# Down projection by Strassen's seven products, with gate and up taken in pairs of column blocks

## The chip, the cores and the metric

The kernel runs on one core of a Trainium2 chip. A core has TensorE (PE in the profile), which multiplies 128x128 stationary by 128x512 moving operands into PSUM; VectorE (DVE), ScalarE (ACT) and GpSimd (POOL) for everything elementwise; and SyncE (SP), whose queue issues all the DMAs of this kernel. The metric is the device time of one execution in microseconds; a time given for a kernel is the median of its runs.

## What is computed

A decoder block over 1024 tokens of 1024 channels, in float32: a gated mixer of pooling and sparse attention, a cross-attention over 256 memory tokens, and a SwiGLU feed-forward layer with 2816 inner columns. The change touches the last alone:

```python
def _swiglu(h, w_gate_up, w_down):
    g, u = jnp.split(h @ w_gate_up, 2, axis=-1)
    return (jax.nn.silu(g) * u) @ w_down
# in reference():
h = _rmsnorm(x, norm_ffn_pre)
x = x + _rmsnorm(_swiglu(h, w_gate_up, w_down), norm_ffn_post)
```

`w_gate_up` is 1024 x 5632 and `w_down` is 2816 x 1024.

## The kernel before

**Numbers in two parts.** TensorE is fed with operands split into a rounded high part and the rest (`split`, line 369: ScalarE copies to the rounded type, VectorE subtracts). A product is three matmuls: high x high, high x low, low x high. So every operand costs one pass on ScalarE and one on VectorE before PE can use it.

**The order of the work.** No instruction is issued where it is written. `Recorder` collects all operations with their dependences; `schedule` then runs a list scheduler with a cost table and writes out one fixed order for each engine's queue. In its table a 128x512 matmul costs 227 ns, a VectorE operation 130 ns and 1.06 ns for each element of a row, and a DMA ends 1300 ns, its bytes at 360 GB/s and another 1300 ns after its issue. At every step it takes the operation that can start first, and among equals the one recorded first. Buffers are rings named by tag: `b` (42 slots of 4 KB a partition, for nearly everything), `ld` (4, raw loads), `wraw` (3, raw weights), `whi`/`wlo` (2 each), `ps1` (4 PSUM banks) and `ps2` (2 pairs of banks). An operation that needs a slot of `b` may be placed at most `AHEAD` = 700 records (`SHORT` = 200 where set) ahead of the oldest one not yet placed, and a ring keeps room for tiles that were recorded earlier (`KEEP`).

**Gate and up** (`gate_up`, line 1195) go over 22 blocks `f` of 128 columns, each by Strassen's seven products in Winograd's form over halves of rows (gate, up), channels and tokens. h3, the normed input, is held for the whole stage as seven operands in both parts, 28 slots of `b`. A block is 7 products of 12 matmuls on three banks `A`, `B`, `C`; `B` and `C` are read by VectorE between two products that accumulate onto the same bank (`u2`, `u3`, `c22`), then `c21 = silu(gate) * up` of the first 512 tokens and `c12` of the last 512 are stored to DRAM in `aTd`. The weight operands of block `f + 1` are made while block `f` runs (`get`, `gu_units`: two loads into `wraw`, four sums, four splits, five slots of `b` and two more for the sums). For the first four blocks they are made far earlier, kept in DRAM (`unitd`, `store`, `fetch`), and the products that use A11 and A12 are done ahead (`gu_first`).

**Down** (line 1239 on) goes over pieces of 2, 4, 4, 4, 4 and 4 of the 22 blocks. In each, both parts of the piece's `w_down` rows (128x1024) and activations (`at`, from `aTd`) stay in slots; for each of 8 token tiles `b` and 2 column halves `n`, PE runs 3 matmuls for each block of the piece into one bank, and VectorE adds the 128x1024 result onto `acc[b]`. In the last piece each half is added, multiplied by the gain `g6`, squared and summed on ScalarE (`jf`), scaled by the root on GpSimd (`mef`, `rf`), added to the residual (`x2r`) and stored.

Of the kernel before, what the change touches and what calls it, by code (L numbers as in the profile page):

```python
# [340 lines left out]
def hybrid_block_kernel(ctx: ExitStack, tc: tile.TileContext, x, mem, norm_mix_pre, norm_mix_post,  # L341
# [544 lines left out]
    def store(f):  # L886

        for j, t in enumerate(gu_units(f)):
            v = f32(t) if len(t.shape) == 3 else f32(t).rearrange("p a c m -> p (a c) m")
            nc.sync.dma_start(unitd[f, j], v)  # L890

    def fetch(f, part):

        ts = []
        nc.ahead = nc.SHORT
        for j in (range(2), range(2, 7))[part]:
            if part == 0:
                t = nc.tile(sb, [P, KC, P], F32R, name=f"uw{f}{j}", tag=("whi", "wlo")[j], bufs=2)
                v = f32(t)
            else:  # L900
                t = slot([P, 2, 4, P], F32R, f"uw{f}{j}")
                v = f32(t).rearrange("p a c m -> p (a c) m")
            nc.sync.dma_start(v, unitd[f, j])
# [164 lines left out]
    for b in range(NB):  # L1068
        mg = nc.tile(sb, [P, KC, P], F32, name=f"mg{b}", tag="ld", bufs=LD)
        nc.sync.dma_start(mg, mgd[:, :, b * P:(b + 1) * P].rearrange("k d t -> d k t"))  # L1070
        mgh, mgl = slot([P, KC, P], F32R, f"mgh{b}"), slot([P, KC, P], F32R, f"mgl{b}")
        split(mgh, mgl, mg, scale=0.5)
        o = bank2([P, 2, 512], f"y{b}")
        tok_gemm(o, lambda c: (mgh[:, c], mgl[:, c]), wo, KC)
        nxt = close(o, x, x1d, b, g2, g3, h2T, "a")
        if pend:
            pend()
        pend = nxt
        if b % 2:
            store(b // 2)  # L1080
    pend()


    aTd = nc.tile(dr, [NF, P, 2, 512], F32, name="aTd", tag="aTd", dram=True)
# [100 lines left out]
    def gu_first(f, W):  # L1185

        A = bank([P, 512], f"ga{f}")
        m = slot([P, 2, 512], F32, f"gm{f}")
        prod(A, W["A11"], "B11", True)
        nc.scalar.activation(m[:, 0], A, AF.Copy)  # L1190
        prod(A, W["A12"], "B21", False)
        nc.scalar.activation(m[:, 1], A, AF.Silu)
        return m[:, 0], m[:, 1]

    def gate_up(f, W, head=None):
        A, B, C = (bank([P, 512], f"g{x}{f}") if head is None or x != "a" else None for x in "abc")
        (m1, u2), (u3, c22), (c12, c21) = ([t[:, j] for j in range(2)] for t in [
            nc.tile(sb, [P, 2, 512], F32, name=f"g{x}{f}", tag="ld", bufs=LD) for x in "muv"])
# [24 lines left out]

    def get(f):
        if f < FIRST:
            return sums(*fetch(f, 1))
        ts = gu_units(f)
        return dict(**own(*ts[:2]), **sums(*ts[2:]))

    head = {f: gu_first(f, own(*fetch(f, 0))) for f in range(FIRST)}  # L1230
    nxt = get(0)
    for f in range(NF):
        cur, nxt = nxt, get(f + 1) if f + 1 < NF else None
        gate_up(f, cur, head.get(f))


    g6 = gain(norm_ffn_post, "g6")
    acc = [None] * NB
    pieces = [range(0, 2)] + [range(f, f + 4) for f in range(2, NF, 4)]
    for fs in pieces:  # L1240
        f0 = fs[0]
        aT, wd = {}, {}
        for f in fs:
            wd[f] = wsplit(wload(w_down[f * P:(f + 1) * P, :], f"wd{f}"), f"wd{f}", keep=True)
            at = nc.tile(sb, [P, 2, 512], F32, name=f"at{f}", tag="ld", bufs=LD)
            nc.sync.dma_start(at, aTd[f])
            nc.ahead = nc.SHORT
            aT[f] = slot([P, 2, 512], F32R, f"aTh{f}"), slot([P, 2, 512], F32R, f"aTl{f}")
            split(*aT[f], at)
            nc.ahead = nc.AHEAD  # L1250
        last = fs[-1] == NF - 1
        for b in range(NB):
            h, t = divmod(b, 4)
            qs = slice(t * P, (t + 1) * P)
            if last:
                o = [bank([P, 512], f"dn{f0}{b}{n}") for n in range(2)]
            else:
                o2 = bank2([P, 2, 512], f"dn{f0}{b}")
                o = [o2[:, n] for n in range(2)]
            for n in range(2):  # L1260
                ns = slice(n * 512, (n + 1) * 512)
                for f in fs:
                    mm3(o[n], aT[f][0][:, h, qs], aT[f][1][:, h, qs], wd[f][0][:, ns], wd[f][1][:, ns],
                        f == fs[0], f == fs[-1])
            if f0 == 0:
                acc[b] = slot([P, D], F32, f"acc{b}")
                nc.vector.tensor_copy(acc[b], o2.rearrange("p n f -> p (n f)"))
            elif not last:
                nc.vector.tensor_tensor(acc[b], o2.rearrange("p n f -> p (n f)"), acc[b], op=OP.add)
            else:  # L1270
                xb = load(x2d[b * P:(b + 1) * P, :], f"x2r{b}")
                ms, z = [], slot([P, D], F32, f"zf{b}")
                for n in range(2):
                    ns = slice(n * 512, (n + 1) * 512)
                    nc.vector.tensor_tensor(acc[b][:, ns], o[n], acc[b][:, ns], op=OP.add)
                    nc.vector.tensor_tensor(z[:, ns], acc[b][:, ns], g6[:, ns], op=OP.mult)
                    m_ = small([P, 1], F32, f"ms{b}{n}")
                    junk = nc.tile(sb, [P, 512], BF, name=f"jf{b}{n}", tag="bf", bufs=2)
                    nc.scalar.activation(junk, acc[b][:, ns], AF.Square, scale=1.0 / 32.0, accum_out=m_)
                    ms.append(m_)  # L1280
                me = small([P, 1], F32, f"mef{b}")
                nc.gpsimd.tensor_scalar(me, ms[0], ms[1], EPS, op0=OP.add, op1=OP.add)
                r = small([P, 1], F32, f"rf{b}")
                nc.gpsimd.tensor_tensor(r, me, mhalf, op=OP.pow)
                for n in range(2):
                    ns = slice(n * 512, (n + 1) * 512)
                    nc.vector.scalar_tensor_tensor(z[:, ns], z[:, ns], r, xb[:, ns], op0=OP.mult, op1=OP.add)
                    nc.sync.dma_start(out[b * P:(b + 1) * P, ns], z[:, ns])

    with tc.manual_schedule():  # L1290
        nc.emit()
# [29 lines left out]
```

## Time and profile before

| | before |
|---|---|
| median of 3 runs | 1612.32 us (1612.13 to 1615.33) |
| the profiled execution, its own time | 1611.7 us |
| its span, first to last instruction | 1609.9 us |
| PE busy, share of the span | 97% |
| DVE busy | 66% |
| ACT busy | 34% |
| DMA moved | 213.16 MB, mean 132 GB/s |

The span is what the trace shows; the rest of the profiled execution's time lies around it. A busy share says how long an engine had an instruction in work. On PE matmuls overlap, so that the listed duration of one is longer than the distance to the next. The granted clock of PE is shown in parts of its full 2.4 GHz. A line number doesn't tell operations apart here, since all are issued through one helper (L139); they are told apart by the names of their tiles.

### The profile page before, as it was taken

The numbers are of one execution on the slowest core, as the hardware profiler recorded it, in microseconds if no ns is written. First come the engines' busy times: TensorE is split into PE (matmuls) and PEld (weight loads), VectorE is DVE, ScalarE is ACT, GpSimd is POOL, SyncE is SP. The second block draws the span as 40 slices with busy tenths as digits, with TensorE's granted clock in tenths as the row PEclk, the third lists the DMA queues.
The fourth block names the chain that finished last, engine by engine and source line by source line (L and its number), as shares of the span: only waits on it lengthen the run. The fifth ranks groups of instructions, "written<-read, shape, count | busy, mean of one in ns | idle before, by whom it ended". The sixth has DMA issues, their size and how long they took to land.

```text
span 1609.9 us, 20252 instructions
## 1 busy us (share of the span) xinstructions
PE 1569.6 (97%) x7590; PEld 1315.9 (82%) x7590; DVE 1054.8 (66%) x1769; ACT 554.4 (34%) x950; POOL 210.1 (13%) x311
## 2 busy tenths in 40 slices
PE   5999999998999999999999999999999999999998
PEld 5877888887888887778899878888888888888886
DVE  6699888989633776468755785755566654644436
ACT  6532111122533655235436661322232222211102
POOL 6055000001232342001103220000000000000001
PEclk9999999999999999999999999999999999999999
DMA  7222412453743232389953356322222225533104
GB/s 224 65 66 68 123 53 66 147 185 116 233 124 92 65 113 79 128 299 370 377 205 106 105 190 216 105 79 80 91 79 83 95 79 162 198 105 105 53 15 157
DMA packets 183683, 213.16 MB, mean 132 GB/s; under 512 B 8600, under 2 KB 141472, under 8 KB 183584
## 3 DMA queue, kind: packets, MB, share of 16 engines
q1 hardware_dynamic: 183584, 211.85, 40.5%
q8 instruction: 60, 0.98, 0.3%
q14 instruction: 39, 0.32, 0.1%
HBM read 148.63 MB, written 63.45 MB: 132 GB/s over the span
## 4 chain that ended last, share of the span: by engine, by line
PE 84%; DVE 7%; issue 4%; DMA 2%; POOL 1%; ACT 1%; SPq 0%; DVEq 0%; POOLq 0%; ACTq 0%
PE dn L139 14%; PE gb L139 11%; PE gc L139 7%; PE ga L139 7%; PE o_q L139 5%; PE o_ga L139 5%; PE o_gp L139 5%; PE o_pa L139 4%; PE y L139 4%; PE po L139 3%; PE lg L139 3%; PE z L139 3%; PE qm L139 3%; PE ap L139 3%; PE pt L139 2%
## 5 line engine op out<-in xcount | busy, mean ns | idle before, releaser
L139 DVE TENSOR_SCALAR_CACHE_REDUCE tja<-score,canda 128x384 bf16<-128x384 f32 (+1 forms) x186 | 165.6, 942 | 0.9
L139 PE MATMUL dn<-h_wd,aTh 128*128 128x512 f32 x352 | 136.8, 389 | 0.0
L139 PE MATMUL dn<-l_wd,aTh 128*128 128x512 f32 x352 | 136.8, 389 | 0.0
L139 PE MATMUL dn<-h_wd,aTl 128*128 128x512 f32 x352 | 136.6, 389 | 0.0
L139 DVE TENSOR_TENSOR acc<-dn,acc 128x1024 f32<-128x1024 f32 (+1 forms) x48 | 50.2, 1047 | 111.6 <-PE dn L139 110.9
L139 POOL TENSOR_SCALAR mef<-ms,ms 128x1 f32<-128x1 f32 x8 | 2.4, 298 | 643.1 <-ACT jf L139 643.1
L139 PEld LDWEIGHTS dn<-h_wd,aTl 128*128 128x128 f32 x352 | 66.1, 188 | 13.8
L139 PEld LDWEIGHTS dn<-l_wd,aTh 128*128 128x128 f32 x352 | 66.1, 188 | 13.8
L139 PEld LDWEIGHTS dn<-h_wd,aTh 128*128 128x128 f32 x352 | 66.1, 188 | 13.5
L139 ACT ACTIVATE h<-s 128x1024 fp32r<-128x1024 f32 x44 | 46.5, 1062 | 82.8 <-DVE s L139 69.1
L139 DVE TENSOR_TENSOR l<-s,h 128x1024 fp32r<-128x1024 f32 x44 | 53.7, 1224 | 31.9 <-PE gc L139 28.1
L139 POOL TENSOR_SCALAR L<-L,ri 128x128 f32<-128x128 f32 (+7 forms) x64 | 48.7, 765 | 175.5 <-DVE ri L139 144.1
L139 PE MATMUL lg<-kTh,qq 128*128 128x512 f32 (+2 forms) x192 | 58.7, 355 | 1.9 <-DVE nn L139 1.3
L139 ACT ACTIVATE aTh<-at 128x1024 fp32r<-128x1024 f32 x22 | 22.8, 1052 | 104.4 <-PE dn L139 94.1
L139 PE MATMUL po<-T,Vh 128*128 128x512 f32 x144 | 55.7, 412 | 2.6 <-DVE T L139 2.5
L139 DVE CUSTOM_DVE_ANT_0 L<-lg,mb 128x256 f32<-128x256 f32 (+1 forms) x64 | 25.5, 402 | 47.8 <-PE lg L139 41.3
L139 DVE TENSOR_TENSOR T<-pt,T 128x512 fp32r<-128x512 f32 x72 | 47.8, 683 | 11.9 <-ACT T L139 11.7
L139 ACT ACTIVATE T<-pt 128x512 fp32r<-128x512 f32 x72 | 40.6, 595 | 34.8 <-PE pt L139 32.4
L139 PE MATMUL y<-h_wo,mgh 128*128 128x512 f32 x128 | 50.4, 394 | 1.4 <-ACT h_wo L139 1.4
L139 ACT ACTIVATE h_wg<-r_wg 128x1024 fp32r<-128x1024 f32 x22 | 23.3, 1061 | 80.2 <-PE ga L139 74.9
L139 PE MATMUL o_ga<-hTh,h_wga 128*128 128x512 f32 x128 | 51.0, 398 | 0.0
L139 POOL TENSOR_TENSOR mb<-Bn,mask 128x1024 f32<-128x1024 f32 (+1 forms) x16 | 34.8, 2174 | 123.8 <-DMA qd<-qh 114.3
(401 smaller groups left out, 4618.1 us busy)
## 6 DMA issues: line engine op xcount, KB each, us to landing
uw<-unitd SPq DMA_DIRECT2D x28, 512.0 KB, 6.0
r_wg<-in_w_gate_up_dram SPq DMA_DIRECT2D x22, 512.0 KB, 4.0
r_wu<-in_w_gate_up_dram SPq DMA_DIRECT2D x22, 512.0 KB, 3.9
aTd<-gv SPq DMA_DIRECT2D x44, 256.0 KB, 2.0
r_wd<-in_w_down_dram SPq DMA_DIRECT2D x22, 512.0 KB, 4.2
at<-aTd SPq DMA_DIRECT2D x22, 512.0 KB, 4.8
qq<-qd SPq DMA_DIRECT2D x32, 256.0 KB, 4.5
r_wpa<-in_w_proj_attn_dram SPq DMA_DIRECT2D x16, 512.0 KB, 4.4
```

The source lines that it names most:

```text
L139: op.emit = lambda: fn(*args, **kw)
```

## The change

Down becomes seven products as well, over halves of the tokens, of DFF (blocks 0 to 10 and 11 to 21) and of the output columns. Each product runs over 11 blocks `k`; for each, it loads one 128x512 block of activations (or of a sum of them) and one of `w_down` (or of a sum of them), splits both at once, and runs 3 matmuls onto each of four banks, one for each tile of 128 tokens. P2 accumulates in the banks of P1 (`A`), P7 and P4 in those of P6 (`B`), and P3 in those of P5 (`C`). P3 runs tile by tile, with all its 11 operands in SBUF, and each tile's closing work stands between.

Gate and up take the blocks in the order 0, 11, 1, 12, and so on. The result tile `c12`, `c21` moves from the `ld` ring to a slot of `b`. After a pair (k, k + 11) four sums of its activations are formed in place on VectorE and stored to DRAM (`act_sums`), next to the blocks that are used as they are; after the first block of a pair four sums of the two `w_down` rows are formed in place and stored (`down_sums`). The diff, cut to its core:

```diff
+    KF = NF // 2
+    ORDER = [k + KF * j for k in range(KF) for j in range(2)]
...
-            nc.tile(sb, [P, 2, 512], F32, name=f"g{x}{f}", tag="ld", bufs=LD) for x in "muv"])
+        (m1, u2), (u3, c22) = ([t[:, j] for j in range(2)] for t in [
+            nc.tile(sb, [P, 2, 512], F32, name=f"g{x}{f}", tag="ld", bufs=LD) for x in "mu"])
+        v = slot([P, 2, 512], F32, f"gv{f}")
+        c12, c21 = v[:, 0], v[:, 1]
...
-        nc.sync.dma_start(aTd[f, :, 0], c21)
+        nc.sync.dma_start(actd["A12" if f >= KF else "A11"][f % KF], c21)
...
-        nc.sync.dma_start(aTd[f, :, 1], c12)
+        if f >= KF:
+            nc.sync.dma_start(actd["A22"][f % KF], c12)
+        return c21, c12
...
+    def act_sums(k, first, second):
+        (A11, A21), (A12, A22) = first, second
+        for n, dst, a, b, op in (("S3", A11, A11, A21, OP.subtract), ("S1", A21, A21, A22, OP.add),
+                                 ("S2", A22, A22, A11, OP.subtract), ("S4", A12, A12, A22, OP.subtract)):
+            nc.vector.tensor_tensor(dst, a, b, op=op)
+            nc.sync.dma_start(actd[n][k], dst)
+
+    def down_sums(k):
+        r = [wload(w_down[f * P:(f + 1) * P, :].rearrange("p (n c) -> p n c", n=2), f"wdr{f}") for f in (k, k + KF)]
+        (B11, B12), (B21, B22) = ([t[:, j] for j in range(2)] for t in r)
+        for n, dst, a, b in (("T1", B11, B12, B11), ("T3", B12, B22, B12), ("T2", B22, B22, B11), ("T4", B21, B21, B22)):
+            nc.vector.tensor_tensor(dst, a, b, op=OP.subtract)
+            nc.sync.dma_start(wdnd[n][k], dst)
...
+    for i, f in enumerate(ORDER):
+        cur, nxt = nxt, get(ORDER[i + 1]) if i + 1 < NF else None
+        got[f] = gate_up(f, cur, head.get(f))
+        if f >= KF:
+            act_sums(f - KF, got.pop(f - KF), got.pop(f))
+        else:
+            down_sums(f)
...
+    SIDE = {"P1": ("A11", "B11"), "P6": ("S2", "T2"), "P2": ("A12", "B21"), "P7": ("S3", "T3"),
+            "P5": ("S1", "T1"), "P4": ("A22", "T4"), "P3": ("S4", "B22")}
+
+    def operands(p, k):
+        a, b = SIDE[p]
+        raw = nc.tile(sb, [P, 2, 512], F32, name=f"dr{p}{k}", tag="ld", bufs=LD)
+        nc.sync.dma_start(raw[:, 0], actd[a][k])
+        if b in wdnd:
+            nc.sync.dma_start(raw[:, 1], wdnd[b][k])
+        else:
+            f, n = k + (KF if b[1] == "2" else 0), int(b[2]) - 1
+            nc.sync.dma_start(raw[:, 1], w_down[f * P:(f + 1) * P, n * 512:(n + 1) * 512])
+        nc.ahead = nc.SHORT
+        hi, lo = slot([P, 2, 512], F32R, f"dh{p}{k}"), slot([P, 2, 512], F32R, f"dl{p}{k}")
+        split(hi, lo, raw)
+        nc.ahead = nc.AHEAD
+        return hi, lo
...
+    def product(p, o, first):
+        for k in range(KF):
+            w = operands(p, k)
+            for t in range(NT):
+                dstep(o[t], w, t, first and k == 0, k == KF - 1)
...
+    A = [bank([P, 512], f"dA{t}") for t in range(NT)]
+    B2 = [bank2([P, 2, 512], f"dB{j}") for j in range(2)]
+    B = [B2[j][:, n] for j in range(2) for n in range(2)]
+    product("P1", A, True)
+    M = [slot([P, 2, 512], F32, f"dm{j}") for j in range(2)]
+    m1 = [M[j][:, n] for j in range(2) for n in range(2)]
+    for t in range(NT):
+        nc.scalar.activation(m1[t], A[t], AF.Copy)
+    product("P6", B, True)
+    for t in range(NT):
+        out_tile(t)
+        nc.vector.tensor_tensor(acc[t][:, half[1]], B[t], m1[t], op=OP.add)
+    product("P2", A, False)
...
+    product("P7", B, False)
...
+    C = [bank([P, 512], f"dC{t}") for t in range(NT)]
+    product("P5", C, True)
...
+    product("P4", B, False)
...
+    ws = [operands("P3", k) for k in range(KF)]
+    for t in range(NT):
+        done(NT + t, 1)
+        done(NT + t, 0)
+        done(t, 0)
+        for k in range(KF):
+            dstep(C[t], ws[k], t, False, k == KF - 1)
+        a = acc[t][:, half[1]]
+        nc.vector.tensor_tensor(a, C[t], a, op=OP.add)
+        done(t, 1)
```

`dstep` is the three matmuls of one token tile; `done(b, n)` is the closing work of one column half of an output tile, with the same operations as before; `out_tile` takes the slot of `acc`.

## Rows read from the trace of the kernel before

**Rows 1.** The page's first part: busy us (share of the span), instructions.
```profile
PE 1569.6 (97%) x7590; PEld 1315.9 (82%) x7590; DVE 1054.8 (66%) x1769; ACT 554.4 (34%) x950; POOL 210.1 (13%) x311
```
**Rows 2.** Windows: stretch, length, busy PE, PEld, DVE, ACT, POOL, clock, DMA share, GB/s.
```profile
600.00:650.00 50.00, 48.96 (x245) 39.93 (x244) 31.76 (x73) 24.15 (x43) 12.16 (x10) 1.00 0.20 66
...
940.00:956.00 16.00, 13.92 (x63) 10.51 (x61) 15.46 (x18) 12.35 (x23) 4.73 (x5) 1.00 0.48 172
...
1030.00:1363.00 333.00, 333.00 (x1471) 275.74 (x1470) 193.53 (x252) 92.77 (x121) 0.00 (x0) 1.00 0.29 92
1363.00:1602.80 239.80, 239.70 (x1058) 198.15 (x1056) 121.15 (x124) 47.34 (x67) 5.99 (x14) 1.00 0.31 107
```
**Rows 3.** The chain that ended last, from 1340 us: start, length, what.
```profile
1360.62 2.72 PE gc L139 x12
1363.34 228.49 PE dn L139 x1008
```
**Rows 4.** Groups of PE: busy us, mean ns; one of down's three alike.
```profile
L139 PE MATMUL dn<-h_wd,aTh 128*128 128x512 f32 x352 | 136.8, 389 | 0.0
```
**Rows 5.** Timeline of PE: start us, length; first and last matmul of down.
```profile
1363.17 0.39 PE L139 MATMUL dn<-h_wd,aTh 128*128 128x512 f32 x1
...
1602.31 0.39 PE L139 MATMUL dn<-h_wd,aTl 128*128 128x512 f32 x1
```
**Rows 6.** Timeline of DVE in one block of gate and up.
```profile
1153.03 0.68 DVE L139 TENSOR_TENSOR s<-r_wg,s 128x512 f32<-128x512 f32 x1
...
1161.87 1.22 DVE L139 TENSOR_TENSOR l<-s,h 128x1024 fp32r<-128x1024 f32 x1 [1.75 <-PE gc L139]
...
1164.82 0.69 DVE L139 TENSOR_TENSOR gu<-gb,gm 128x512 f32<-128x512 f32 x1 [1.12 <-PE gb L139]
```
**Rows 7.** DMA from 1030 to 1363 us; an issue's row ends with us to landing.
```profile
DMA packets 36803, 30.65 MB, mean 92 GB/s; under 512 B 1200, under 2 KB 30896, under 8 KB 36786
...
aTd<-gv SPq DMA_DIRECT2D x35, 256.0 KB, 2.0
```
**Rows 8.** DMA from 684 to 805 us, the most crowded stretch.
```profile
DMA packets 30817, 42.17 MB, mean 349 GB/s; under 512 B 1396, under 2 KB 22270, under 8 KB 30809
...
mg<-mgd SPq DMA_DIRECT2D x8, 512.0 KB, 8.4
...
unitd<-l_wg SPq DMA_DIRECT2D x4, 512.0 KB, 9.3
```
**Rows 9.** Groups of DVE, then of ACT, from 1363 us to the end.
```profile
L139 DVE TENSOR_TENSOR aTl<-at,aTh 128x1024 fp32r<-128x1024 f32 x21 | 25.5, 1218 | 0.0
...
L139 DVE SCALAR_TENSOR_TENSOR zf<-zf,rf,x2r 128x512 f32<-128x512 f32 x16 | 11.3, 745 | 1.2 <-POOL rf L139 1.2
L139 DVE TENSOR_TENSOR acc<-dn,acc 128x512 f32<-128x512 f32 x16 | 11.1, 692 | 12.6 <-PE dn L139 11.9
...
L139 ACT ACTIVATE aTh<-at 128x1024 fp32r<-128x1024 f32 x20 | 20.7, 1051 | 100.9 <-PE dn L139 94.1 <-DMA at<-aTd 6.8
```
**Rows 10.** Timeline of SP's queue, two loads of down's second piece.
```profile
1387.52 0.33 SPq L139 DMA_DIRECT2D r_wd<-in_w_down_dram  x1
1388.65 0.32 SPq L139 DMA_DIRECT2D at<-aTd  x1
```
**Rows 11.** DMA issues from 1363 us to the end.
```profile
at<-aTd SPq DMA_DIRECT2D x20, 512.0 KB, 4.9
...
aTd<-gv SPq DMA_DIRECT2D x1, 256.0 KB, 5.5
```
**Rows 12.** DMA from 1387 to 1400 us, those loads and six more.
```profile
DMA packets 1030, 3.78 MB, mean 291 GB/s; under 512 B 111, under 2 KB 111, under 8 KB 1029
```
**Rows 13.** Timeline of PE where matmuls of two banks alternate.
```profile
645.01 0.40 PE L139 MATMUL o_pa<-atl,h_wpa 128*128 128x512 f32 x1
645.25 0.39 PE L139 MATMUL po<-T,Vh 128*128 128x512 f32 x1
```

More of the change, by code (lines that the diff above doesn't have):

```diff
@@ L902, in fetch @@
                 v = f32(t).rearrange("p a c m -> p (a c) m")
-            nc.sync.dma_start(v, unitd[f, j])
+            nc.sync.dma_start(v, unitd[ORDER.index(f), j])
             ts.append(t)
@@ L1079, in hybrid_block_kernel @@
         if b % 2:
-            store(b // 2)
+            store(ORDER[b // 2])
     pend()
-    aTd = nc.tile(dr, [NF, P, 2, 512], F32, name="aTd", tag="aTd", dram=True)
     KVm = [slot([P, D], F32R, f"{n}n{w}_") for n in "KV" for w in "hl"]
@@ L1221, in gate_up @@
         nc.vector.tensor_tensor(c12, c12, c22, op=OP.mult)
-        nc.sync.dma_start(aTd[f, :, 1], c12)
+        if f >= KF:
+            nc.sync.dma_start(actd["A22"][f % KF], c12)
+        return c21, c12
+    actd = {n: nc.tile(dr, [KF, P, 512], F32, name=f"act{n}", tag=f"act{n}", dram=True)
+            for n in ("A11", "A12", "A22", "S1", "S2", "S3", "S4")}
+    wdnd = {n: nc.tile(dr, [KF, P, 512], F32, name=f"wdn{n}", tag=f"wdn{n}", dram=True)
+            for n in ("T1", "T2", "T3", "T4")}
+    def act_sums(k, first, second):
[10 more added lines that the diff above has]
+            nc.sync.dma_start(wdnd[n][k], dst)
     def get(f):
-        if f < FIRST:
+        if f in ORDER[:FIRST]:
             return sums(*fetch(f, 1))
@@ L1228, in get @@
         return dict(**own(*ts[:2]), **sums(*ts[2:]))
[L1230 to L1234, printed above, removed]
-    g6 = gain(norm_ffn_post, "g6")
[L1238 to L1288, printed above, removed]
@@ new lines, in hybrid_block_kernel @@
+    head = {f: gu_first(f, own(*fetch(f, 0))) for f in ORDER[:FIRST]}
+    nxt = get(ORDER[0])
+    got = {}
+    for i, f in enumerate(ORDER):
[5 more added lines that the diff above has]
+            down_sums(f)
+    g6 = gain(norm_ffn_post, "g6")
+    NT = 4
+    acc = {}
+    SIDE = {"P1": ("A11", "B11"), "P6": ("S2", "T2"), "P2": ("A12", "B21"), "P7": ("S3", "T3"),
+            "P5": ("S1", "T1"), "P4": ("A22", "T4"), "P3": ("S4", "B22")}
@@ new lines, in dstep @@
+    def dstep(o, w, t, first, last):
+        hi, lo = w
+        q = slice(t * P, (t + 1) * P)
+        nc.tensor.matmul(o, hi[:, 0, q], hi[:, 1], start=first, stop=False, skip_group_check=True)
+        nc.tensor.matmul(o, hi[:, 0, q], lo[:, 1], start=False, stop=False, skip_group_check=True)
+        nc.tensor.matmul(o, lo[:, 0, q], hi[:, 1], start=False, stop=last, skip_group_check=True)
+    def product(p, o, first):
[3 more added lines that the diff above has]
+                dstep(o[t], w, t, first and k == 0, k == KF - 1)
@@ new lines, in out_tile, with done @@
+    def out_tile(b):
+        acc[b] = slot([P, D], F32, f"acc{b}")
+    half = [slice(n * 512, (n + 1) * 512) for n in range(2)]
+    zs, sums_of = {}, {}
+    def done(b, n):
+        if b not in zs:
+            zs[b], sums_of[b] = slot([P, D], F32, f"zf{b}"), []
+        z, ns = zs[b], half[n]
+        nc.vector.tensor_tensor(z[:, ns], acc[b][:, ns], g6[:, ns], op=OP.mult)
+        m_ = small([P, 1], F32, f"ms{b}{n}")
+        junk = nc.tile(sb, [P, 512], BF, name=f"jf{b}{n}", tag="bf", bufs=2)
+        nc.scalar.activation(junk, acc[b][:, ns], AF.Square, scale=1.0 / 32.0, accum_out=m_)
+        sums_of[b].append(m_)
+        if len(sums_of[b]) == 1:
+            return
+        xb = load(x2d[b * P:(b + 1) * P, :], f"x2r{b}")
+        ms = sums_of[b]
+        me = small([P, 1], F32, f"mef{b}")
+        nc.gpsimd.tensor_scalar(me, ms[0], ms[1], EPS, op0=OP.add, op1=OP.add)
+        r = small([P, 1], F32, f"rf{b}")
+        nc.gpsimd.tensor_tensor(r, me, mhalf, op=OP.pow)
+        for j in range(2):
+            js = half[j]
+            nc.vector.scalar_tensor_tensor(z[:, js], z[:, js], r, xb[:, js], op0=OP.mult, op1=OP.add)
+            nc.sync.dma_start(out[b * P:(b + 1) * P, js], z[:, js])
@@ new lines, in hybrid_block_kernel @@
+    product("P2", A, False)
+    for t in range(NT):
+        nc.scalar.activation(acc[t][:, half[0]], A[t], AF.Copy)
+    product("P7", B, False)
+    for t in range(NT):
+        out_tile(NT + t)
+        nc.vector.tensor_tensor(acc[NT + t][:, half[1]], B[t], m1[t], op=OP.add)
+    C = [bank([P, 512], f"dC{t}") for t in range(NT)]
+    product("P5", C, True)
+    for t in range(NT):
+        a = acc[NT + t][:, half[1]]
+        nc.vector.tensor_tensor(a, C[t], a, op=OP.add)
+    product("P4", B, False)
@@ L1290, in hybrid_block_kernel @@
+    for t in range(NT):
+        nc.vector.tensor_tensor(acc[NT + t][:, half[0]], B[t], m1[t], op=OP.add)
+    ws = [operands("P3", k) for k in range(KF)]
+    for t in range(NT):
+        done(NT + t, 1)
[4 more added lines that the diff above has]
+        a = acc[t][:, half[1]]
+        nc.vector.tensor_tensor(a, C[t], a, op=OP.add)
+        done(t, 1)
     with tc.manual_schedule():
```

5 lines of the change are left out of this document (3 added, 2 removed).

## The prediction, made before the change was run

> **What bounds the kernel now.** I read the busy share of each engine first [rows 1]: TensorE (PE) is busy for 97% of the span of 1609.9 us, VectorE (DVE) for 66%. A busy share is an average, so the stretches that the change touches come next [rows 2]. From 1030 to 1363 us (most of gate and up) and from 1363 to 1602.8 us (down) PE is busy all the time at a granted clock of 1.00, that is at the 2.4 GHz level, while DVE works 193.5 of 333 us and 121.2 of 239.8 us. The chain of waits says the same [rows 3]: gate/up goes through it in pieces of 12 matmuls and 2.72 us with nothing between, and down is one piece of PE. So in both stretches only one thing sets the time: how many matmuls there are, and how far apart they start.
>
> That distance isn't the duration in the table of groups. A down matmul is listed with 389 ns [rows 4], but its successor starts long before it ends. From the first to the last down matmul [rows 5] it is 1602.31 - 1363.17 = 239.14 us for 1055 steps: 226.7 ns each. The 12 matmuls in 2.72 us of gate/up give the same 226.7 ns. This is the price I use; 389 ns would overstate every saving by 72%.
>
> **What the change takes away.** Down now does, for each of 22 blocks of DFF, 8 token tiles, 2 column halves and 3 matmuls (hi x hi, hi x lo, lo x hi): 22 x 8 x 2 x 3 = 1056. Seven products over halves are 7 x 11 blocks x 4 token tiles x 3 = 924. That is 132 fewer, with the same 128x512 shape: 132 x 0.2267 = 29.9 us. PE's down stage becomes 924 x 0.2267 = 209.5 us. Gate and up keep their matmuls: `ORDER` changes only which block comes when.
>
> **What it adds in gate/up, and what hides it.** For each pair of blocks DVE gets four sums of activations and four of `w_down`, all 128x512 in SBUF. The like subtraction of the weight units takes 0.68 us [rows 6], so 8 x 0.68 = 5.5 us for each pair. A pair lasts 2 x 7 products x 2.72 = 38.1 us, and DVE's share there goes from 58% (193.5 / 333) to 73%. Cover: PE's own work. DVE must read a bank between two products that use it (`u2` before S3's product accumulates onto the same bank): one product, 2.72 us, in which the read takes 0.69 us [rows 6]. A split (1.23 us) or a sum in front of it still fits, so I cost this at nothing; if the cover were gone, all of it on the path would be 11 x 5.5 = 60 us.
>
> The sums are in place, which adds a wait: S2 overwrites the tile from which block A22 is being stored, so DVE must wait until that store has landed. Behind it on DVE stand S2, S4 and whatever comes next, among it the bank reads for which PE waits. Such a store takes 2.0 us from issue to landing now [rows 7]. The planner that sets the order reckons a store's end by 1.3 us twice plus its bytes, 3.3 us, and puts the sum only then; nothing should stand. Bound: 0 to 16 us, the upper end in the rivals. I take 0, since the 2.0 us row is this very store.
>
> The tile `gv` leaves the four-deep ring of `ld` for the 42 slots, and lives until both blocks of the pair are done. By the code h3's operands hold 28 slots, the running unit 5, the next one 7 with its sums; two `gv` make 42. Exactly full, so a next unit may come later than now. It has room: its `l<-s` at 1161.87 us [rows 6] is for a product that starts some 19 us later, a whole block of 84 matmuls. Cost nothing; a block's delay over that would be seen at once as PE idle.
>
> DMA in gate/up grows for each pair by two `w_down` rows of 512 KB, four sums and three activation blocks of 256 KB, 2.9 MB in 38.1 us or 76 GB/s; the queues run at 92 GB/s there [rows 7] and reach 349 elsewhere [rows 8]. Hidden. A few sums of the first pairs may slip into DVE's busy end of the memory sub-layer, where PE already loses 2.1 of 16 us [rows 2]: 0 to 2 us, and a shift there could also gain those 2 us. I take 0.
>
> **What it adds in down.** Each of the 77 operand pairs needs two loads of 256 KB, a split on ScalarE (ACT, 1.05 us) and one on DVE (1.22 us) [rows 9], and feeds 12 matmuls: 2.72 us of PE. Sums over the stage: DVE 77 x 1.22 = 94, 20 bank reads x 0.69 = 14, and the closing sixteen multiplies (0.69) and sixteen fused ops (0.745) = 23 [rows 9]: 131 of 209 us, 62%. Now it is 121 of 240 us, 51% [rows 2]: the splits double, and the wide accumulations of every piece go. ACT 77 x 1.05 = 81 us, with eight copies and the sixteen squares as now some 100 of 209 us. The SP queue issues a load in 0.33 us [rows 10]: 154 x 0.33 = 51 us. None is a bound by its sum.
>
> The supply has one narrow place: raw operands go through the four `ld` buffers. One buffer's turn is two issues 0.65 us, landing 4.9 us (the median of `at<-aTd` in this stage [rows 11]; two of half the size may be quicker or slower), splits 1.05 + 1.22 us, and about 0.4 us for hops: 8.2 us. Four in 8.2 us is one in 2.06 us, against a need of one in 2.72. Three quarters, so operands run ahead of PE, as deep as slots allow (42 less 8 `acc`, 2 `dm`, 1 `g6`). P3 needs all eleven within its first 7.5 us; 22 of the 31 slots hold them. Bytes: 0.524 MB in 2.72 us is 193 GB/s; the trace has 291 GB/s over 13 us of this stage [rows 12], with loads of 512 KB 1.13 us apart [rows 10], and 349 GB/s over 121 us [rows 8]. I take no cost.
>
> Banks: P2 and P7 accumulate onto what P1 and P6 left, and each read of a bank has the whole next product (30 us) before its bank is written. At the seam, `dA3` waits for the last read of gate/up (0.69 us), and nine matmuls, 2.0 us, stand in front of it. P1's left side (blocks 0 to 10) is complete one block before gate/up ends. The tail, 7.6 us from the last matmul's start [rows 5] to the end of the span (read, multiply, square, two on GpSimd, two fused, store), has the same instructions as now.
>
> **Sum.** The profiled execution took 1611.7 us, 1.8 us of it outside its span, and is 0.6 us below the median of 1612.32. 1611.7 - 29.9 = 1581.8 us; against the median 1582.4. I say 1582.5.
>
> **Rivals.** (a) *Gate/up stutters.* The A22 store lands as late as the slow one now seen (5.5 us, `aTd<-gv` at the busy seam [rows 11]) and DVE stands 3.5 us longer in each pair. The read that comes next has 2.72 - 0.69 = 2.0 us to spare, so PE loses 1.5 us, eleven times: 16 us, 1598.9 us. For it: a strict queue, and SP may hold the store behind a load that waits. Against: the planner's 3.3 us, the low DMA share.
>
> (b) *The operand ring is late, up to slower than before.* A turn may take 4 x 2.72 = 10.9 us without loss, a landing of 7.6 us. In the crowded stretch loads of 512 KB land in 8.4 us [rows 8]: a turn of 11.7 us, 2.93 us for each operand, 77 x 0.21 = 16 us lost, 1598.6 us. It decides at 239.4 / 77 = 3.11 us, a turn of 12.4 us, a landing of 9.1 us; at the 9.3 us of that stretch's slowest group [rows 8] a turn is 12.6 us, 3.155 us for each operand and 242.9 us for down: 33.4 us lost, 1615.8 us, slower than before. Against: that stretch moves 349 GB/s with all DMA engines busy, and down asks for 193. The Trainium skill, "DMA: Bandwidth & Descriptors", section Bandwidth, advises batches of at least 1 MiB for three quarters of the peak; by that rule loads cut to a quarter of one would fall short of the need and the time would be that of (b). It was measured on another issue path, and here the trace speaks against it: 512 KB loads overlap to 291 GB/s [rows 12].
>
> (c) *The array's clock falls.* The change goes to another PSUM bank every 3 matmuls instead of every 6 or 12. If PE had small gaps there and its granted clock fell to the 1.2 GHz level, down would take up to twice 209.5 us: slower as soon as 14% of down (29.9 / 209.5) ran at that level, 1792 us if all did. Against: at 645 us matmuls of two banks alternate with starts 0.23 us apart [rows 13], in a stretch with clock 1.00 [rows 2]. The Trainium skill, "TensorE: Matmul & The Clock Gate", section "A second HAM failure mode: psum-queue depth-cycling", describes a kernel that lost its clock by cycling through banks at each step; by that, (c) would hold, and the trace doesn't bear it out.
>
> (d) *Nothing is gained*: P3, which needs eleven operands in SBUF at once, waits for them as long as the 132 matmuls took, 1609 to 1616 us. Its 22 slots of 31 speak against it, and so does that operands run ahead all through P4.
>
> **Chances.** Forecast, 1579.5 to 1586: 0.74. (a) and the mild half of (b), 1586 to 1605: 0.17. Below 1579.5: 0.02. (b) over its point: 0.04; (c) 0.01; (d) 0.02. The range, 1579.5 to 1600, takes in the two bounds of 16 us. 0.2%, 3.2 us, is about what a measurement of this kernel can tell from no change: faster 0.93, same 0.02, slower 0.05.
>
> **What the profile after would show.** Right: 924 down matmuls, first to last start 209.3 us, steps of 226.7 ns, no PE wait from the start of gate/up to the last matmul, DVE near 73% in gate/up and 62% in down. Wrong: PE waiting in gate/up for a bank whose DVE read stands behind S2 (a); PE waiting for `dl` or `dh` with landings over 7.6 us (b); a granted clock below 1.00 in down (c).

## The result and the profile after

The changed kernel takes 1588.82 us (1586.52 to 1589.61, 4 runs) where the kernel before takes 1612.22 us (1610.47 to 1615.33, 4 runs of the same comparison): a ratio of 0.985, with a 95% interval of 0.9832 to 0.9869. That is 23.4 us less; the prediction had 29.9 us less, and lies 6.3 us below the measured time. Its sign and its range held; its middle did not.

The page of after, first part, answers to [rows 1]: 132 matmuls fewer (7590 to 7458), and 27.1 us less of busy PE.

```profile
PE 1542.5 (97%) x7458; PEld 1292.9 (82%) x7458; DVE 1099.4 (69%) x1854; ACT 595.7 (38%) x991; POOL 214.7 (14%) x311
```

The windows of gate/up and of down in after, with the columns of [rows 2]:

```profile
1030.00:1363.00 333.00, 333.00 (x1470) 275.81 (x1469) 229.90 (x320) 94.14 (x121) 0.00 (x0) 1.00 0.47 156
1363.00:1577.00 214.00, 210.71 (x926) 173.19 (x925) 123.02 (x126) 90.36 (x111) 11.08 (x14) 1.00 0.66 219
```

Gate/up is as it was: PE busy for 333.00 of 333 us, clock 1.00, although DVE works 36 us more there (193.5 in [rows 2], 229.9 here). Down is not: 3.29 us of 214 us of PE are missing, where before 0.1 of 239.8 us was. The ends of down in the timeline of PE, to set beside [rows 5]:

```profile
1363.46 0.39 PE L139 MATMUL dA<-dhP 128*128 128x512 f32 x1
...
1577.16 0.39 PE L139 MATMUL dC<-dhP,dlP 128*128 128x512 f32 x1
```

From first to last start it is 213.70 us; 923 steps of 226.7 ns would be 209.24. So 4.46 us of the missing 6.5 (29.9 forecast, 23.4 measured) are inside down. What PE waited for there is one row of its waits (total us, times, longest); the second row is a wait in the memory sub-layer, 1.04 us of it at 882.76 us, that was 0.2 us, once, before:

```profile
PE dB L139 <- DVE acc L139: 3.3, 4, 0.9
...
PE mo L139 <- DVE mT L139: 1.2, 2, 1.0
```

`acc<-dB` is the read with which VectorE takes a finished product out of a bank. The timeline of PE at the end of P6, and then that of DVE, show the two stops of that product (P7 has two more, at 1484.59 and 1487.04 us):

```profile
1421.26 0.39 PE L139 MATMUL dB<-dhP 128*128 128x512 f32 x1
1422.58 0.50 PE L139 MATMUL dB<-dlP,dhP 128*128 128x512 f32 x1 [0.94 <-DVE acc L139]
...
1423.87 0.39 PE L139 MATMUL dB<-dhP 128*128 128x512 f32 x1
1425.04 0.50 PE L139 MATMUL dB<-dlP,dhP 128*128 128x512 f32 x1 [0.78 <-DVE acc L139]
```

```profile
1421.84 0.68 DVE L139 TENSOR_TENSOR acc<-dB,dm 128x512 f32<-128x512 f32 x1
1423.36 0.69 DVE L139 TENSOR_TENSOR acc<-dB,dm 128x512 f32<-128x512 f32 x1 [0.84 <-PE dB L139]
```

The last block of P6 (k = 10) goes through the token tiles one after another, three matmuls each. The tile `B2[0]` holds the banks of token tiles 0 and 1, `B2[1]` those of 2 and 3. When token tile 0 is finished DVE reads it at 1421.84 us; PE has one matmul of token tile 1 out (1421.26) and does not issue the next until the read is over (1422.58). The same happens with tiles 2 and 3. Between two starts lie 1.32 and 1.17 us instead of 0.227, and the next few are 0.34 and 0.24 us apart: P6 takes 32.2 us (first `dB` at 1393.38, first `dA` at 1425.60) instead of 29.92. The waiting goes both ways. Token tile 2 has its last matmul at 1423.63 us, which ends at 1424.03; its read starts only at 1424.29, when the first matmul of tile 3, in the other bank (1423.87 and 0.39 long), has ended. P4, in the same tiles, has no stop: its four reads run one after another from 1546.30 us, each behind the last matmul of its pair.

Two explanations for the 6.5 us stood open then. Mine: four stops by reads of a neighbour bank (4.5 us), and the rest from sums that land in the memory sub-layer. The rivals: the work added in gate/up and the added operand traffic (the sums, DVE at 69%, the ring), with the stops a mere symptom of a DVE that is late.

### The profile page after: what moved, and what is told of

It is laid out like the page before. It is cut to its first block, busy times and chain, and to the rows that moved or that the text cites. A ratio compares the mean times of both kernels' runs of the same rounds, so it can differ in the third digit from the quotient of the medians.

```text
span 1584.7 us, 20558 instructions
## 1 busy us (share of the span) xinstructions
PE 1542.5 (97%) x7458; PEld 1292.9 (82%) x7458; DVE 1099.4 (69%) x1854; ACT 595.7 (38%) x991; POOL 214.7 (14%) x311
## 4 chain that ended last, share of the span: by engine, by line
PE 79%; DVE 8%; DMA 5%; issue 4%; ACT 2%; POOL 1%; SPq 1%; DVEq 0%; POOLq 0%; ACTq 0%
PE gb L139 11%; PE gc L139 8%; PE ga L139 7%; PE o_q L139 5%; PE o_ga L139 5%; PE o_gp L139 5%; PE y L139 4%; PE dB L139 4%; PE o_pa L139 4%; PE dC L139 3%; PE po L139 3%; PE lg L139 3%; PE ap L139 3%; PE qm L139 3%; PE z L139 2%
## 5 line engine op out<-in xcount | busy, mean ns | idle before, releaser
L139 DVE TENSOR_TENSOR dlP<-drP,dhP 128x1024 fp32r<-128x1024 f32 x77 | 94.0, 1224 | 61.9 <-ACT dhP L139 27.0
L139 ACT ACTIVATE dhP<-drP 128x1024 fp32r<-128x1024 f32 x77 | 81.6, 1061 | 82.4 <-PE dB L139 25.5
L139 POOL TENSOR_SCALAR mef<-ms,ms 128x1 f32<-128x1 f32 x8 | 6.8, 855 | 612.5 <-ACT jf L139 612.2
L139 PE MATMUL dB<-dlP,dhP 128*128 128x512 f32 x132 | 51.8, 392 | 3.3 <-DVE acc L139 3.3
L139 PE MATMUL dB<-dhP,dlP 128*128 128x512 f32 x132 | 51.4, 389 | 0.0
L139 PE MATMUL dB<-dhP 128*128 128x512 f32 x132 | 51.4, 389 | 0.0
L139 PE MATMUL o_ga<-hTl,h_wga 128*128 128x512 f32 x128 | 50.8, 397 | 0.0
L139 PE MATMUL y<-l_wo,mgh 128*128 128x512 f32 x128 | 50.0, 390 | 0.8 <-DVE l_wo L139 0.8
L139 PE MATMUL o_ga<-hTh,l_wga 128*128 128x512 f32 x128 | 50.5, 395 | 0.0
L139 PE MATMUL o_pa<-ath,h_wpa 128*128 128x512 f32 x128 | 50.3, 393 | 0.0
```

What stands on the lines that cost most here:

```text
L139: op.emit = lambda: fn(*args, **kw)
```

## The experiments

**Run again.** The changed kernel as it is, beside the first three experiments.

> The changed kernel once more, unchanged, beside the others on the same chip. Both theories: 1587 to 1590 us. Its second profile says which part of the missing 6.5 us (29.9 forecast, 23.4 measured) is always there: four stops of PE at the reads of bank pairs in P6 and P7 (0.8 to 0.9 us each, PE waiting for DVE acc) should stand in it again; if the profiled time is 2 us longer than the first profile's 1586.5, the rows that differ name the rest.

1589.72 us (1586.53 to 1591.36), ratio 0.9858 (0.984 to 0.9876); down from first to last start 213.6 us, `mo` 1.1 us. The profiled execution was the slowest, and its first down matmul started at 1368.43 us instead of 1363.46; 4.8 of these 5 us stand there already at the last `qm` matmul, before gate/up begins. So two executions of one kernel differ by some us. This is why the parts below are read from stretches of the trace, and the times only confirm them.

**Reads at the product's end.** The four reads of P6, P7 and P4 are planned behind the product's last matmul; the rest is as it was. `deps` counts in the planner alone: it puts the reads later in the order and adds no wait on the chip.

```diff
-    product("P6", B, True)
+    end = product("P6", B, True)          # the same for P7 and P4
...
-        nc.vector.tensor_tensor(acc[t][:, half[1]], B[t], m1[t], op=OP.add)
+        nc.vector.tensor_tensor(acc[t][:, half[1]], B[t], m1[t], op=OP.add).deps.add(end)
```

> One edit: the reads of the banks of P6, P7 and P4 are planned after the product's last matmul, not after the last matmul of each bank. Theory (the four stops come from reads that stand between two matmuls onto halves of one pair tile, though they touch different banks): the stops vanish, 4 x (0.83 + 0.16) = 4.0 us, so 1584.8 us where the changed kernel has 1588.8. Rival (P1 and P6 are held by the operand ring anyway, since the chain of waits runs through loads there): the time comes back as waits for the split operands, and the kernel stays within 1 us of the changed one.

1582.63 us (1581.35 to 1583.81), ratio 0.9816 (0.9801 to 0.9832). The chain of this kernel (start, length, what) is seven products of one length, back to back:

```profile
1364.74 29.92 PE dA L139 x132
1394.66 29.92 PE dB L139 x132
1424.58 29.92 PE dA L139 x132
1454.50 29.92 PE dB L139 x132
1484.42 29.92 PE dC L139 x132
1514.34 29.92 PE dB L139 x132
1544.26 22.45 PE dC L139 x99
```

and its window from the first down matmul to the last has no gap, with DVE at 59%:

```profile
1364.58:1573.79 209.21, 209.21 (x924) 173.24 (x923) 122.90 (x126) 90.28 (x111) 10.12 (x14) 1.00 0.67 223
```

209.21 us is the prediction's 209.3, with all sums, loads and splits in place. So the stops are 4.5 us of the loss, and the same reads behind the matmuls cost nothing. In after the chain runs through loads, splits and the read up to the first stop (1421.84 us), yet PE waits there for no load. A late DVE has at most 0.15 us in it: the first stop of after (1.32 us from start to start, where the other three have 1.17), whose read came behind a split. The two times differ by 6 to 7 us, more than the 4.5 us of the trace; the rest is no more than executions of one kernel differ by.

The reads don't wait for the product's end, though. The timeline of PE at the end of P6, the last matmuls of token tiles 1 and 3, and then DVE's first read:

```profile
1422.84 0.39 PE L139 MATMUL dB<-dhP,dlP 128*128 128x512 f32 x1
...
1424.19 0.39 PE L139 MATMUL dB<-dhP,dlP 128*128 128x512 f32 x1
```

```profile
1423.26 0.69 DVE L139 TENSOR_TENSOR acc<-dB,dm 128x512 f32<-128x512 f32 x1 [1.98 <-PE dB L139]
```

The read of token tile 0 starts when the last matmul of its pair has ended (1422.84 + 0.39), while PE works on the other pair and goes on without a gap. What costs is a read planned between two matmuls onto one pair. Run a second time:

> The kernel with the reads planned last, again, as the neighbour on the same chip for the one that also holds the first sums back. 1581 to 1584 us; from the last qm matmul to the first gb matmul 157.4 to 158.2 us.

1583.63 us (1582.53 to 1588.13), ratio 0.9827 (0.9807 to 0.9847), 209.2 us again.

**Is it the bank, the tile or the product?** First the banks were dealt out to the token tiles in another order, so that the neighbours of one tile are 0 and 2, 1 and 3:

```diff
-    B = [B2[j][:, n] for j in range(2) for n in range(2)]
+    B = [B2[j][:, n] for n in range(2) for j in range(2)]
```

> The changed kernel with one line different: the four banks of B are taken in the order pair 0, pair 1, pair 0, pair 1 instead of 0, 0, 1, 1. Theory (a matmul waits for the read of the other half of its own pair): in P6 and P7 the read of the first tile now has three matmuls onto the other pair in front of the one that must wait, so each of the four stops shrinks from 1.1 us (start to start, above the pace) to about 0.4 us, 1.6 us in all instead of 4.4. Rival (a matmul waits for whatever bank read was issued before it, or for the engine that reads): four stops of the old size. Time of one look, 1584 to 1589 us, says little.

1586.17 us, one run. With three matmuls of the other tile between a read and the next matmul onto its neighbour, P6 and P7 take 30.33 us each (0.4 over the pace; P6 of after 2.3), with one short stop each where I had expected two; but P4, which had no stop, now has two of this kind (1544.67 and 1546.43 us), and down takes 212.3 us from first to last start. PE's waits from 1340 us on have one row:

```profile
PE dB L139 <- DVE acc L139: 1.6, 2, 0.8
```

That pointed to the pair of banks in one tile, but DVE stood differently too. So the two kinds of tile were exchanged: pairs for P1, P2, P5 and P3, single banks for P6, P7 and P4.

```diff
-    A = [bank([P, 512], f"dA{t}") for t in range(NT)]
-    B2 = [bank2([P, 2, 512], f"dB{j}") for j in range(2)]
-    B = [B2[j][:, n] for j in range(2) for n in range(2)]
+    A2 = [bank2([P, 2, 512], f"dA{j}") for j in range(2)]
+    A = [A2[j][:, n] for j in range(2) for n in range(2)]
+    B = [bank([P, 512], f"dB{t}") for t in range(NT)]      # dC in pairs, as dA
```

> The changed kernel with the accumulators of P1, P2, P5 and P3 in the two tiles of two banks and those of P6, P7 and P4 in four tiles of one bank; nothing else differs. If the stop belongs to the tile (a read of one half of a pair holds up matmuls onto the other half, whichever product it is): none at the ends of P6, P7 and P4, P6 and P7 at 29.9 us, and new ones at the ends of P1, P2 and P5, where ScalarE's copies (0.58 us) or VectorE's adds of one half stand before matmuls onto the other half, 2 to 4 us for each of these products because ScalarE may be in a split of 1.06 us first; down 213 us or more. If it belongs to these products (the read itself, VectorE's load there): the four stops at P6 and P7 remain, 213.2 us, and P1, P2 and P5 stay at 29.9 us.

1586.07 us, one run. PE's waits from 1340 us on:

```profile
PE dC L139 <- DVE acc L139: 1.6, 2, 0.8
PE dA L139 <- ACT dm L139: 0.7, 1, 0.7
PE dA L139 <- ACT acc L139: 0.7, 1, 0.7
```

None for `dB`: P6, P7 and P4 run at 29.92 us, though DVE's first read of P7 starts at 1483.14 us and P7 runs to 1484.98: a read of a bank that is a tile of its own, in the middle of the product, stops nothing. The stops went with the pairs, and with them from DVE's reads to ScalarE's copies in P1 and P2. Timeline of ACT, then of PE, at the end of P1:

```profile
1391.65 0.60 ACT L139 ACTIVATE dm<-dA 128x512 f32<-128x512 f32 x1 [0.27 <-PE dA L139]
```

```profile
1392.30 0.50 PE L139 MATMUL dA<-dlP,dhP 128*128 128x512 f32 x1 [0.69 <-ACT dm L139]
```

There are four stops again and down takes 213.4 us, but not where I had placed all of them: one each in P1 and P2 (in P1 the third copy runs only at 1394.44 us, when token tile 3 is through), two in P3, none in P5, and P1 and P2 lose 1.0 us each, not 2 to 4. The theory of the tile held; which of a pair's reads fall between its matmuls depends on what the reading engine has in front of them.

The Trainium skill, "PSUM — Partial Sum Buffer", section "PSUM bank collisions raise a hardware error", asks to guard PSUM by bank and quadrant. By that rule a read of one half (128x512 float32, a bank) and matmuls onto the other half need no order between them; the waits here cover the tile of two banks, which is more than the rule asks.

**Gate/up alone.** Down as before, gate/up with pairs, sums and stores (A21 is stored too, which before is read).

> Only the gate/up half of the change: pairs of blocks, the tile in a slot, all eight sums formed and stored (the stored sums are then not used), and down as in the kernel before, with its 1056 matmuls, loading activations from the new places. Theory (the added DVE work and the in-place waits are hidden behind PE): 1612 us, that of the kernel before, within 1.5 us. Rival (gate/up pays part of the missing 6.5 us): 1614 to 1616 us, with PE waits between the start of gate/up and its end.

1614.18 us, ratio 1.0009 (0.9999 to 1.0019). In its window gate/up loses nothing, with DVE at 71%. What it may lose, 0 to 3 us, lies ahead of that: PE waits 1.0 us for `mT` in the memory sub-layer, as in after.

```profile
1030.00:1363.00 333.00, 333.00 (x1471) 275.74 (x1470) 236.26 (x327) 98.07 (x125) 0.00 (x0) 1.00 0.52 176
```

**No sums.** The eight sums of each pair and their stores are left out, and down reads plain blocks in their place; PE's work is that of after.

```diff
-        if f >= KF:
-            act_sums(f - KF, got.pop(f - KF), got.pop(f))
-        else:
-            down_sums(f)
...
-    SIDE = {"P1": ("A11", "B11"), "P6": ("S2", "T2"), "P2": ("A12", "B21"), "P7": ("S3", "T3"),
-            "P5": ("S1", "T1"), "P4": ("A22", "T4"), "P3": ("S4", "B22")}
+    SIDE = {"P1": ("A11", "B11"), "P6": ("A22", "B22"), "P2": ("A12", "B21"), "P7": ("A11", "B12"),
+            "P5": ("A22", "B12"), "P4": ("A22", "B21"), "P3": ("A12", "B22")}
```

> The changed kernel without its eight sums for each pair: no adds, no stores of them, no first load of w_down; the seven products read plain blocks in their place (the sums are left out of what is computed), with the same 924 matmuls. Theory (sums hidden): within 1 us of the changed kernel, 1588 us. Rival (sums cost): 2 to 6 us faster than it.

1586.63 us (1585.86 to 1587.37), ratio 0.9841 (0.9827 to 0.9856): without the sums there is 2 to 3 us, not 6.5. Its waits in down are those of after, its `mo` wait is 0.2 us as before:

```profile
PE dB L139 <- DVE acc L139: 3.1, 4, 0.8
```

So the four stops are not the sums' doing, and the sums cost something ahead of gate/up. From the start of the last `qm` matmul to the first of down it is 495.70 us in before and 495.65 here, but 496.9 to 497.9 in all nine executions shown here that have the early sums (after and the reads at the end twice each, gate/up alone, the banks in another order, the exchanged tiles, the two rings below): 1.2 to 2.2 us. (An expectation below has 496.0 for before; by the two starts it is 495.70.) The T sums of the first two pairs run on DVE from 865 to 882 us there, among the operations for which the memory sub-layer's `mo` product waits. The timeline of DVE in after, then that of PE, show the wait of 1.04 us: DVE stands 3.43 us for a load of `w_down` rows, does three sums, and `mT` is behind them.

```profile
879.96 1.42 DVE L139 TENSOR_TENSOR r_wdr<-r_wdr,r_wdr 128x512 f32<-128x512 f32 x2 [3.43 <-DMA r_wdr<-in_w_down_dram]
881.41 0.69 DVE L139 TENSOR_TENSOR r_wdr<-r_wdr 128x512 f32<-128x512 f32 x1
882.02 0.68 DVE L139 TENSOR_TENSOR mT<-mpt,mT 128x512 fp32r<-128x512 f32 x1
```

```profile
882.76 0.39 PE L139 MATMUL mo<-mT,Vnh__1659 128*128 128x256 f32 x1 [1.04 <-DVE mT L139]
```

**Sums later.** With the reads at the ends, the T sums are planned behind gate/up's first S2 product (`begun["mm"]` is its last matmul).

```diff
-            nc.vector.tensor_tensor(dst, a, b, op=OP.subtract)
+            nc.vector.tensor_tensor(dst, a, b, op=OP.subtract).deps.add(begun["mm"])
```

> The reads planned last, as in the kernel that removed the four stops, and one more edit: the w_down sums of the first pairs may not start before gate/up's first S2 product has ended (in the changed kernel two pairs of them run at 865 to 882 us, between the memory sub-layer's VectorE work). Theory (they cost 1.4 to 2.2 us there: from the last qm matmul to the first gb matmul of gate/up it is 155.8 to 156.0 us without them, 157.4 to 158.2 with them): that stretch returns to 156 us and the kernel is 1.5 to 2 us faster than the one with the reads alone, about 1581 us. Rival (the sums only move: the first self-made weight unit then waits for the raw-weight ring behind them): the same time or slower, with a PE wait near 1022 us.

1584.97 us (1581.96 to 1586.64), ratio 0.983 (0.9812 to 0.9847): no gain to be seen. The `mo` wait is back at 0.2 us, but a stop of 0.97 us is new, in the first pair. Timeline of DVE, then of PE:

```profile
984.54 0.69 DVE L139 TENSOR_TENSOR r_wdr<-r_wdr 128x512 f32<-128x512 f32 x1
987.32 0.69 DVE L139 TENSOR_TENSOR gv<-gv 128x512 f32<-128x512 f32 x1 [2.08 <-DMA actA<-gv]
987.92 1.22 DVE L139 TENSOR_TENSOR l_wg<-r_wg,h_wg 128x1024 fp32r<-128x1024 f32 x1
989.06 0.68 DVE L139 TENSOR_TENSOR gu<-gb,gm 128x512 f32<-128x512 f32 x1
```

```profile
988.44 0.39 PE L139 MATMUL gb<-h3T2l,uw 128*128 128x512 f32 x1
989.80 0.50 PE L139 MATMUL gb<-h3T4h,uw 128*128 128x512 f32 x1 [0.97 <-DVE gu L139]
```

This is rival (a) of the prediction in kind, once (the sum is S3 or S4, within one block's tile, and not S2): an in-place sum waits 2.08 us for the store of its tile to land, a split follows, and the bank read behind both comes late. From the last `qm` to down it is 496.66 us, 0.2 to 1.3 us less than theirs. One more place, then: after the first add into c22, one product later.

```diff
-        nc.vector.tensor_tensor(c22, C, u3, op=OP.add)
+        begun.setdefault("c22", nc.vector.tensor_tensor(c22, C, u3, op=OP.add))
...
-            nc.vector.tensor_tensor(dst, a, b, op=OP.subtract)
+            nc.vector.tensor_tensor(dst, a, b, op=OP.subtract).deps.add(begun["c22"])
```

> The reads of P6, P7 and P4 wait for their product's end, and the T sums may not start on VectorE before gate/up's first add into block 22 (the first run of that line), one product later than in e4. My theory (the sums cost what stands behind them on VectorE while TensorE needs a read): neither the memory sub-layer nor the first pair is stopped. The stop of TensorE for mT is back at 0.2 us, that for gu (1.0 us in e4) is gone, last memory-sub-layer score to first down matmul 495.8 to 496.2 us (before: 496.0), down 208.7 us: about 1581 us, 1 us below e4 and 1 to 2 below e1. Rival (there is no free place for the sums of the first two pairs: they only move): a new stop of about 1 us for another read in the first pair or near 1022 us, where the first own units start; 1583, as e1.

Neither stop is left (no wait for `gu`; `mo` 0.2 us), and the stretch is 495.76 us, that of before. The timeline of PE, at its two ends:

```profile
869.14 0.28 PE L139 MATMUL qm<-h2h,l_wqm 128*128 128x256 f32 x1
...
1364.90 0.39 PE L139 MATMUL dA<-dhP 128*128 128x512 f32 x1
```

So this trace shows the sums at no cost, against the rival. The time, 1582.95 us (1580.51 to 1584.75), ratio 0.9803 (0.9784 to 0.9822), doesn't prove it: the 1 to 2 us expected against the kernel with early sums are within the spread, and the last `qm` came 1 to 2.5 us later in this execution than in theirs.

**The operand ring.** With the reads at the ends, the raw operands go through two buffers (the ring of `whi`), and in another kernel through three (that of `wraw`), instead of four.

```diff
-        raw = nc.tile(sb, [P, 2, 512], F32, name=f"dr{p}{k}", tag="ld", bufs=LD)
+        raw = f32(nc.tile(sb, [P, 2, 512], F32R, name=f"dr{p}{k}", tag="whi", bufs=2))
# and in the other kernel
+        raw = nc.tile(sb, [P, 2, 512], F32, name=f"dr{p}{k}", tag="wraw", bufs=3)
```

> The kernel with the reads planned last, with the raw operands of down in a ring of two buffers instead of four. By the working of the prediction a buffer's turn is 8.2 us, so an operand would come every 4.1 us and down would take 77 x 4.1 = 316 us, 106 us more. By the chain of the changed kernel, where turns of 5.7 to 8.8 us follow each other with 7.0 us in the mean, it is 3.5 us, 270 us, 60 us more. With fewer loads in flight each may land earlier, then less. Rival (the ring isn't what paces the loads): the time stays, 1583 us.

> The raw operands of down go through a ring of three buffers (with the reads at the products' ends). By the prediction's turn of 8.2 us an operand comes every 2.73 us against a need of 2.72: just at break-even, down 209 to 211 us, and 1 to 8 us more if the turns of the crowded beginning (up to 8.8 us) held all through. By the shorter turn that the ring of two showed (5.7 us, landings 2.7 us), 1.9 to 2.3 us for each operand: no wait for dh or dl after P1, down 208.7 us, about 1583 us as with four. If the landing of a load does not depend on how many are under way, the first holds.

Two buffers: 1613.97 us, down 232.5 us, 23 us more than with four. PE is listed busy for 220.7 us of it. So 11.8 of the 23 us are idle time, and the rest lies in the matmuls around the waits, which start further apart than the pace. The first rows of its waits in down:

```profile
PE dC L139 <- ACT dhP L139: 4.7, 6, 1.6
PE dB L139 <- DVE dlP L139: 2.6, 4, 0.8
```

Three buffers: 1583.02 us, no wait, and the window of down is the full pace:

```profile
1364.45:1573.66 209.21, 209.21 (x925) 173.24 (x923) 115.83 (x121) 84.71 (x106) 10.12 (x14) 1.00 0.64 204
```

By the prediction's turn of 8.2 us two buffers would give an operand every 4.1 us, 77 x 4.1 = 316 us for down, and three would sit at the break-even of 2.72. It was 232.5 us, 77 x 3.02, a turn of some 6 us. The loads account for it: with a landing of 2.8 us in place of 4.9 the prediction's sum for a turn is 6.1 us. An operand load (256 KB, last number: median us to landing) in the crowded first part of down in after (1363 to 1430 us, 286 GB/s), and then with two buffers (from 1430 us on):

```profile
drP<-actS SPq DMA_DIRECT2D x19, 256.0 KB, 4.2
drP<-wdnT SPq DMA_DIRECT2D x19, 256.0 KB, 4.6
```

```profile
drP<-actS SPq DMA_DIRECT2D x33, 256.0 KB, 2.7
drP<-wdnT SPq DMA_DIRECT2D x33, 256.0 KB, 2.9
```

The two stretches differ, so compare like with like: in the first part of down (1363 to 1430 us) two buffers move 200 GB/s and their loads land in 2.6 to 3.5 us; from 1430 to 1545 us, at 187 GB/s, the four of after land theirs in 2.7 to 3.7 us. So here a load landed sooner where less was moving, and a short ring pays less than its number of buffers says. Two are too few, three are enough, and the four of the change have room.

## Why the prediction was right, and where it was off

**What held, and what was luck.** The sign and the range (1579.5 to 1600) held. The forecast proper, 1579.5 to 1586 with a chance of 0.74, did not: 1588.82 us lies above it, where the prediction had put rival (a) and the mild half of (b), and the range reached that far for these two alone. Neither came. The time got there by waits that the prediction had set at nothing, so that the range held it is luck.

**The price of a matmul held.** 226.7 ns from start to start and 132 matmuls fewer give 29.9 us; without stops down takes 209.21 us, to 0.1 us what the sum had. The 389 ns of [rows 4] would have promised 51 us.

**The step that failed is "Banks".** It says that each read of a bank has the whole next product before its bank is written, and so costs nothing. By banks that is true. But P6, P7 and P4 accumulate into tiles of two banks, and a read of one half holds up the matmuls onto the other half, which are still to come in the same product. I had asked who writes this bank next, not who writes this tile next. A term of 0 was 4.46 us, two thirds of what was missing: shown by the reads at the ends (the stops go), by the exchanged tiles (they move with the pairs) and by the kernel without sums (they stay). It could have been asked from the code: `B2` and `B` stand side by side in the diff, and `[:, n]` of a tile is no tile. The profile that the prediction foretold, with no PE wait up to the last matmul, is not that of after, and none of its three signs of being wrong names such a wait.

**"0 to 2 us … I take 0"**, for sums that slip into the memory sub-layer, was 1.2 to 2.2 us in that stretch, of which 1.0 is the row of `mo`. The two longest stretches (497.9 us with the reads at the ends, 497.8 with gate/up alone) also wait 0.9 us instead of 0.4 for the stored units (`ga` for `uw<-unitd`); what causes that was not tried. The bound was right but for 0.2 us, the choice was the wrong end of it. The row it rested on pointed the other way: DVE busy 15.46 of 16 us from 940 to 956 [rows 2]. The first sums went to 865 us, earlier than I looked, where DVE reads for PE as well.

Together 4.46 + 1.2 to 2.2 = 5.7 to 6.7 us, beside the measured 6.5 (29.9 - 23.4). What is left is below what executions of one kernel differ by.

**Gate/up hid its work**, as costed: no wait of PE from 1030 us to its end, at 69% of DVE instead of 73% (in down 59% without stops, instead of 62%). Two assumptions under it were too kind. Stores land later than the 2.0 us of [rows 7], while the queues move 156 GB/s instead of 92. The DMA issues of after from 1030 to 1363 us:

```profile
actS<-gv SPq DMA_DIRECT2D x35, 256.0 KB, 4.5
...
actA<-gv SPq DMA_DIRECT2D x26, 256.0 KB, 2.7
```

And "nothing should stand" is wrong: DVE did wait for those stores, though never so long that PE did. The groups of DVE there, with the idle time ahead of them at the end:

```profile
L139 DVE TENSOR_TENSOR gv<-gv 128x512 f32<-128x512 f32 x18 | 12.4, 688 | 1.1 <-DMA actA<-gv 0.8
...
L139 DVE TENSOR_TENSOR gv<-gv,gv 128x512 f32<-128x512 f32 x17 | 11.7, 687 | 6.0 <-DMA actA<-gv 6.0
```

This is the wait of rival (a), but 6.8 us over the window are 0.8 us for each pair and not its 3.5; in after it fell into DVE's spare time, and where the T sums were moved next to it, it cost PE 1 us once.

**Rival (b)**, the ring, stayed away: landings of 4.2 to 4.6 us where 7.6 was the break-even. Its direction was right (two buffers lose 23 us); its size was too large, because a landing taken from a busy stretch is not a constant. **Rival (c)**, the clock: a granted clock of 1.00, the 2.4 GHz level, in every window of down shown here, with a change of bank every three matmuls; it is 1.00 over the 232.5 us with two buffers too, where PE waits 17 times (11.2 us in all). The Trainium skill ("TensorE: Matmul & The Clock Gate", section "A second HAM failure mode: psum-queue depth-cycling") tells of a kernel that cycled through banks, stood idle for short times between groups of matmuls, and whose clock went up and down by it; neither the full pace nor these waits lowered it here. **Rival (d)**: P3's 33 matmuls for each token tile ran without a wait for an operand. **The tail** is 7.5 us, as before.

## What to carry to other kernels

When an accumulator is finished bank by bank, ask which tile its banks belong to: here a read of one bank of a pair, planned between two matmuls onto the other, stopped TensorE for the length of the read and some 0.4 us around it. Plan the reads behind the last matmul onto the pair, or give each bank a tile of its own. And work that is "hidden" under a full engine must not only fit by its sum: look where the scheduler can put its first pieces, at both ends of the stretch that is meant to hide it.

## What the runs showed that was not expected

- A stop of PE by a 0.69 us read costs 1.1 us against the pace (4.46 / 4): 0.78 to 0.94 us idle, and the first matmul after it lasts 0.50 us instead of 0.39 and is followed 0.34 us later instead of 0.227. The stops' listed 3.3 us are 4.46 us of time. In the 1.17 us between two starts lie the whole 0.39 us of the matmul before, the read, and 0.09 us between the three.
- In the same stretch of down (1363 to 1430 us) 256 KB loads landed in 2.6 to 3.5 us with two buffers in the ring (200 GB/s), in 3.5 to 4.1 with three (249 GB/s) and in 4.2 to 4.6 with four (286 GB/s): a deeper ring lengthened its own landings.
- What sets the waits on the pair was not tried. The kernel's planner keeps the halves of a tile apart (`_region` and `_hit` compare ranges of elements), and so could put a read between two matmuls onto the other half; whether the waits come from how the program tracks its tiles behind the planner, or from something else, stays open. The runs show only that they follow the tile, in both directions.
